# Split SiLU-multiply: each partition's rows in HBM, from one 64 KiB piece per tile to eight adjacent pieces taken by eight tiles

## The chip, the cores and the metric

The kernel runs on one core of one Trainium2 chip. The metric is the device time of one execution in microseconds; the time before is the median of three runs. A profile is one more execution, recorded by the hardware profiler.

## The reference

The input x has the shape (32, 512, 2048) in float32, 16384 rows of 8 KiB, 134.22 MB. The output has 1024 columns, 67.11 MB.

```python
def reference(x):
    half_dim = x.shape[-1] // 2
    x1, x2 = (x[..., :half_dim].copy(), x[..., half_dim:].copy())
    silu_x1 = x1 * (1 / (1 + np.exp(-x1)))
    return (silu_x1 * x2).astype(np.float32)
```

Each row is treated by itself, so it does not matter for the result which row lies on which partition, as long as the output goes to the row that the input came from.

## The kernel before

The 16384 rows are cut into 16 tiles of 1024 rows (8 MiB of x, 4 MiB of out). A tile gives K = 8 rows to each of the 128 partitions. The function `view` says which: tile i is the block of 1024 adjacent rows from row 1024 i, and partition p takes the eight adjacent rows from 8 p in it. So a partition's part of a tile is one run of 64 KiB of x, and the next partition's run follows it without a gap; a whole tile is one run of 8 MiB. In out the same holds with half the bytes, 32 KiB and 4 MiB.

There are two input buffers (`xts`) and two output buffers (`ots`), taken in turn. For each tile there is one load on SyncE's queue (in `load`, by `move`, L87), SiLU in place on the first half of each row on ScalarE (L103), the multiply with the second half into the output buffer on VectorE (L109), and one store on ScalarE's queue (in `store`, by `move`, L87). The first tile is computed in four parts and stored in five pieces (`OPENING`), which take the partitions in steps of four or two; the last is computed and stored in two parts. The other 14 tiles are each one activation, one multiply and one store.

The order on ScalarE and VectorE is written out by hand (`manual_schedule`). A load of tile i + 2 waits for the multiply of tile i, which frees its input buffer; a multiply of tile i + 2 waits for the store of tile i, which frees its output buffer. In turns of four tiles the load of tile i + 2 is ordered before or behind the store of tile i (`load_first`, `after`). Declarations of waits that are implied by others (`implied`) keep the number of semaphores down. At the end SyncE waits for the transfers to land.

Of the kernel before, what the change touches and what calls it, by code (L numbers as in the profile page):

```python
# [1 line left out]

# [4 lines left out]


@with_exitstack
def kernel(  # L10
    ctx: ExitStack,
    tc: tile.TileContext,
    x: bass.AP,
    out: bass.AP,
):


    nc = tc.nc
    P = nc.NUM_PARTITIONS

    x_flat = x.flatten_outer_dims()
    out_flat = out.flatten_outer_dims()
    num_rows, in_cols = x_flat.shape
    half = in_cols // 2
    dt = x_flat.dtype

    K = 8
    KC_EDGE = 2
    KS = 4
    OPENING = [  # L30
        (slice(0, None, 4), slice(0, 2)),
        (slice(2, None, 4), slice(0, 4)),
        (slice(2, None, 4), slice(4, None)),
        (slice(0, None, 4), slice(2, None)),
        (slice(1, None, 2), slice(None)),
    ]
    PLAN = [K] * (num_rows // (P * K))

    pool = ctx.enter_context(tc.tile_pool(name="pool", bufs=1))
    xts = [pool.tile([P, K, in_cols], dt, name=f"xt{b}") for b in range(2)]  # L40
    ots = [pool.tile([P, K, half], dt, name=f"ot{b}") for b in range(2)]

    plan = []
    row = 0
    for k in PLAN:
        plan.append((row, k))
        row += P * k
    assert row == num_rows
    n_tiles = len(plan)

    def view(flat, i):
        row0, k = plan[i]
        return flat[row0:row0 + P * k].rearrange("(p k) d -> p k d", k=k)

    ctx.enter_context(tc.manual_schedule(engines={mybir.EngineType.Activation, mybir.EngineType.DVE}))

    sent = []
    loads, stores, silus, muls = {}, {}, {}, {}

    def implied(later, earlier, reason):  # L60
        for x in later:
            for y in earlier:
                tc.declare_no_dep(x, y, reason=reason)

    def earlier(done, i):
        return [ins for j in range(i % 2, i, 2) for ins in done[j]]

    def after(later, first):
        tc.add_manual_dep(
            later,  # L70
            first.name,
            mybir.DependencyInfo(mybir.DependencyClass.NoSync, mybir.DependencyReason.DATA),
            reason="order in which the transfers take their semaphores",
        )

    def settle_all_but(n):
        rest = nc.sync.nop(nofuse=True)
        for ins in sent[:-n]:
            tc.add_manual_dep(
                rest.ins,  # L80
                ins.name,
                mybir.DependencyInfo(mybir.DependencyClass.Sync, mybir.DependencyReason.DATA),
                reason="sync sees each earlier transfer land before the last ones",
            )

    def move(queue, out, in_):
        ins = queue.dma_start(out=out, in_=in_).ins  # L87
        sent.append(ins)
        return ins

    def load(i):
        loads[i] = [move(nc.sync, xts[i % 2][:], view(x_flat, i))]
        if i >= 2:
            implied(loads[i], earlier(loads, i), "the multiplies that this load awaits came after those loads")
            implied(loads[i], earlier(silus, i), "the multiplies that this load awaits came after those activations")

    def compute(i, ot, kc):
        xt = xts[i % 2]
        silus[i], muls[i] = [], []
        for c in range(0, K, kc):  # L100
            ks = slice(c, c + kc)
            silus[i].append(
                nc.scalar.activation(  # L103
                    out=xt[:, ks, :half],
                    in_=xt[:, ks, :half],
                    func=mybir.ActivationFunctionType.Silu,
                ).ins
            )
            muls[i].append(nc.vector.tensor_mul(out=ot[:, ks], in0=xt[:, ks, :half], in1=xt[:, ks, half:]).ins)  # L109
        implied(muls[i], loads[i], "each multiply awaits an activation that came after the load")  # L110
        if i >= 2:
            implied(silus[i], earlier(silus, i), "the load that this activation awaits came after those activations")
            implied(silus[i], earlier(muls, i), "the load that this activation awaits came after those multiplies")
            implied(muls[i], earlier(muls, i), "the store that this multiply awaits came after those multiplies")

    def store(i, ot, pieces):
        ov = view(out_flat, i)
        stores[i] = [move(nc.scalar, ov[ps, ks], ot[ps, ks]) for ps, ks in pieces]

    ALL = slice(None)  # L120
    load(0)
    load(1)
    for i in range(n_tiles):
        ot = ots[i % 2]
        last = i == n_tiles - 1
        compute(i, ot, KC_EDGE if i == 0 else KS if last else K)
        pieces = [(ALL, ALL)]
        if i == 0:
            pieces = OPENING
        elif last:  # L130
            pieces = [(ALL, slice(c, c + KS)) for c in range(0, K, KS)]
        load_first = i // 4 % 2
        if load_first and i + 2 < n_tiles:
            load(i + 2)
        store(i, ot, pieces)
        if load_first and i + 2 < n_tiles:
            after(stores[i][0], loads[i + 2][0])
        if not load_first and i + 2 < n_tiles:
            load(i + 2)
            after(loads[i + 2][0], stores[i][-1])  # L140
    settle_all_but(1)


# [1 line left out]
_INS = ['x']  # L145
_OUTS = [((32, 512, 1024), 'float32')]


# [23 lines left out]
```

## Time and profile before

| what | value |
|---|---|
| median of 3 runs | 470.68 us (470.57 to 470.76) |
| profiled execution | 471.83 us |
| its span, first to last instruction | 470.1 us |
| VectorE busy | 139.3 us, 30% of the span |
| ScalarE busy | 114.1 us, 24% |
| loads' queue (q1) | 134.22 MB, 66.2% of 16 DMA engines' span |
| stores' queue (q10) | 67.11 MB, 33.1% |
| mean rate of HBM traffic | 428 GB/s over the span |
| activation of a whole tile | 7.03 us |
| multiply of a whole tile | 8.69 us |

The page gives the busy time of each engine, the share of the DMA engines in 40 slices of the span, and the queues; the trace behind it can be asked for windows of time, for waits and for the chain of work that ended last. The trace also has one record for each packet that a DMA engine moved: its start, its duration and its bytes. A load has 128 data packets of 64 KiB, a whole store 128 of 32 KiB.

### The profile page before, as it was taken

To read this page: it belongs to the slowest core of one execution; us is meant where nothing else is said; L and a number is where in the kernel's file an instruction comes from. 1 tells how busy PE (TensorE), PEld (TensorE's weight loads), DVE (VectorE), ACT (ScalarE), POOL (GpSimd) and SP (SyncE) were. 2 spreads that over 40 slices of the span, in tenths; PEclk is the share of its full clock that TensorE was granted. 3 is DMA by queue.
4 is the path that set the end of the run, shared out by engine and by line. 5 is a ranking of instruction groups with operands and counts; after the bars stand their busy time and mean duration, and the time that the engine had idled before them with its cause. 6 is when DMAs were issued, how large, how long until landed. Compare 5 with 4: busy or idle time off the path is not lost.

```text
span 470.1 us, 157 instructions
## 1 busy us (share of the span) xinstructions
DVE 139.3 (30%) x20; ACT 114.1 (24%) x21; POOL 0.2 (0%) x4
## 2 busy tenths in 40 slices
DVE  0070614307042070520605116060150702507061
ACT  1052305050040501405014050230503205032060
POOL 0000000000000000000000000000000000000000
DMA  8999999999999999999999999999999999999997
GB/s 357 446 468 424 402 441 404 415 480 402 446 402 485 407 421 427 485 407 402 443 446 443 407 443 488 393 415 443 482 407 446 404 429 460 407 446 421 424 425 336
DMA packets 4880, 201.33 MB, mean 428 GB/s; under 512 B 592, under 2 KB 592, under 8 KB 592
## 3 DMA queue, kind: packets, MB, share of 16 engines
q1 hardware_dynamic: 2304, 134.22, 66.2%
q10 hardware_dynamic: 2576, 67.11, 33.1%
HBM read 134.22 MB, written 67.11 MB: 428 GB/s over the span
## 4 chain that ended last, share of the span: by engine, by line
DMA 80%; DVE 14%; ACT 2%; DVEq 1%; issue 0%; SPq 0%
DMA out_dram<-ot 62%; DMA xt<-in_x_dram 18%; DVE ot L109 14%; ACT xt L103 2%; DVEq L167 1%; SPq L87 0%; DVEq L109 0%
## 5 line engine op out<-in xcount | busy, mean ns | idle before, releaser
L109 DVE TENSOR_TENSOR ot<-xt 128x8192 f32<-128x8192 f32 (+2 forms) x20 | 139.3, 6984 | 320.5 <-DMA out_dram<-ot 180.1
L103 ACT ACTIVATE xt<-xt 128x8192 f32<-128x8192 f32 (+2 forms) x20 | 112.8, 5661 | 339.7 <-DMA xt<-in_x_dram 339.7
L103 ACT ACT_TABLE_LOAD x1 | 1.3, 1283 | 0.7 <-PEq L156 0.7
L156 POOL MEMSET const-bfloat16-1.0<- 128x1 bf16 x1 | 0.1, 102 | 0.0
L156 POOL MEMSET const-uint8-127<- 128x1 uint8 x1 | 0.1, 102 | 0.0
L156 POOL MEMSET const-float32-0.0<- 128x1 f32 x1 | 0.1, 99 | 0.2 <-issue 0.2
L156 POOL MEMSET const-float32-1.0<- 128x1 f32 x1 | 0.1, 99 | 0.0
## 6 DMA issues: line engine op xcount, KB each, us to landing
out_dram<-ot ACTq DMA_DIRECT2D x14, 4096.0 KB, 49.2
out_dram<-ot ACTq DMA_DIRECT2D x3, 2048.0 KB, 9.4
out_dram<-ot ACTq DMA_DIRECT2D x2, 512.0 KB, 17.3
out_dram<-ot ACTq DMA_DIRECT2D x1, 768.0 KB, 28.1
xt<-in_x_dram SPq DMA_DIRECT2D x16, 42.1
out_dram<-ot ACTq DMA_DIRECT2D x1, 256.0 KB, 10.9
```

Of the source, the lines that this page charges most:

```text
L103: nc.scalar.activation(out=xt[:, ks, :half], in_=xt[:, ks, :half], func=mybir.ActivationFunctionType.Silu,).ins
L109: muls[i].append(nc.vector.tensor_mul(out=ot[:, ks], in0=xt[:, ks, :half], in1=xt[:, ks, half:]).ins)
L156: nc = _bacc.Bacc("TRN2", target_bir_lowering=False, num_devices=1)
L167: with _tile.TileContext(nc) as tc:
```

## The change

The 16 tiles remain, with the same shapes, buffers and order. `view` now cuts the 16384 rows into two groups of 8192 rows (64 MiB of x). In a group a partition owns 64 adjacent rows, 512 KiB of x, as eight pieces of eight rows; tile t of the group takes piece t of every partition. A partition's part of a tile is still one run of 64 KiB of x and 32 KiB of out, but the next partition's run now begins 512 KiB further on in x, and 256 KiB further on in out. The list of tiles with their first rows (`PLAN`, `plan`) goes, as the view works the addresses out from the tile's number.

```diff
-    PLAN = [K] * (num_rows // (P * K))
+    RUN = 8
+    n_tiles = num_rows // (P * K)
...
-    plan = []
-    row = 0
-    for k in PLAN:
-        plan.append((row, k))
-        row += P * k
-    assert row == num_rows
-    n_tiles = len(plan)
-
     def view(flat, i):
-        row0, k = plan[i]
-        return flat[row0:row0 + P * k].rearrange("(p k) d -> p k d", k=k)
+        return flat.rearrange("(g p t k) d -> g t p k d", p=P, t=RUN, k=K)[i // RUN, i % RUN]
```

## The prediction

> **What bounds the kernel now.** I read the page first, its parts 1 to 3.
>
> ```profile
> span 470.1 us, 157 instructions
> DVE 139.3 (30%) x20; ACT 114.1 (24%) x21; POOL 0.2 (0%) x4
> ...
> DMA  8999999999999999999999999999999999999997
> ...
> q1 hardware_dynamic: 2304, 134.22, 66.2%
> q10 hardware_dynamic: 2576, 67.11, 33.1%
> ```
>
> The two compute engines stand idle for over two thirds of the span. The sixteen DMA engines are busy 66.2% + 33.1% = 99.3% of it: 311.2 us with loads (queue q1) and 155.6 us with stores (q10), together 466.8 us of 470.1. The missing 3.3 us lie at the two ends of the span. So the time is the sum of the packets that one DMA engine handles, and the question is whether a packet can become shorter or longer. The view by windows says at which rate they run:
>
> ```profile
> 0.00:13.00 13.00, 0.00 (x0) 1.28 (x1) 0.20 (x4) 1.00 0.99 403
> 44.00:60.00 16.00, 8.62 (x1) 7.03 (x1) 0.00 (x0) 1.00 0.96 410
> 86.00:144.00 58.00, 17.39 (x2) 14.06 (x2) 0.00 (x0) 1.00 1.00 434
> 144.00:202.00 58.00, 16.99 (x2) 14.06 (x2) 0.00 (x0) 1.00 1.00 434
> 376.00:434.00 58.00, 17.37 (x3) 14.06 (x2) 0.00 (x0) 1.00 1.00 434
> 434.00:470.00 36.00, 9.18 (x3) 7.12 (x2) 0.00 (x0) 1.00 0.91 394
> ```
>
> The last two columns are the DMA engines' share and the GB/s. From 86 to 434 us the rate is 434 in each 58 us, whatever the mixture of loads and stores. The trace's own packet records show how flat this is: most 64 KiB load packets took 2.418 us, to the nanosecond, and most 32 KiB store packets 1.213 us. A memory that was short of something would scatter these numbers. What scatter there is lies nearly all ahead of 62 us: the first sixteen load packets (2.96 to 3.35 us, mean 3.140), and two later batches of sixteen that start together at 37 and 61 us (means 2.740 and 2.745). Summed over all packets, the time above 2.418, 1.213 and the like is 1.72 us for each engine.
>
> Last, the waits, to see who would notice a longer packet:
>
> ```profile
> ACT xt L103 <- DMA xt<-in_x_dram: 339.7, 16, 22.4
> DVE ot L109 <- DMA out_dram<-ot: 180.1, 9, 20.8
> DVE ot L109 <- ACT xt L103: 140.4, 7, 24.6
> ```
>
> ACT waits for a load before each tile, some 22 us long, and DVE for a store or for ACT. Nothing in compute can give time back: a microsecond more of packets on one engine is a microsecond more of span.
>
> **The change part by part.** The instruction streams stay as they are: each engine has the same instructions in the same order with the same shapes (16 loads of 128 x 16384 elements, 14 full stores, 7 pieces), only their source lines move up by eight. So no instruction, wait or DMA issue is added, removed or moved: cost nothing, and no cover is needed. Packet sizes stay too: a partition's part of a tile is still one run of 64 KiB of x and 32 KiB of out, and the bytes are still 134.22 + 67.11 MB. The floor stays at 128 load packets x 2.418 = 309.5 us for an engine plus its stores.
>
> What moves is the address. In a load, neighbouring partitions lay 64 KiB apart and now lie 512 KiB apart; in a store 32 KiB becomes 256 KiB. Whichever partitions the sixteen engines serve at a moment, their addresses differed by multiples of 64 KiB and now differ by multiples of 512 KiB: three more low address bits are equal in all sixteen streams, and the engines run in step, since their first packets all started within 0.4 us and then took equal times. If the memory spreads addresses over its channels by those bits, streams meet on a channel, and the packets get longer. The opening stores go over every fourth partition, so their runs lie 1 MiB apart, but they are 4.19 MB in all, 9.7 us at 434 GB/s; a tenth more there is 1 us, and I give them no term.
>
> No row of before shows a packet at the new distance, so I bound it. Below nothing: all of today's scatter goes, -1.72 us. Zero: 2.418 us as now. Above: each of the 128 load packets of an engine costs what the restarted batches cost, (2.740 + 2.745) / 2 - 2.418 = 0.324 us more, together 41.5 us; or, furthest, what the first sixteen cost, 0.722 us more, together 92.4 us. For stores the row is 1.213 us with nothing above 1.225, and their distance grows only to 256 KiB, so I take zero there. For loads I choose near the lower end, because 434 GB/s is held without scatter over 350 us, so the memory has something to spare: the restart price on one packet in eight, the first of every load, where the sixteen streams jump together by a new base. That is 16 x 0.324 = 5.2 us. It is a choice between bounds and not a measurement.
>
> One rule of the notes speaks against the change. The Trainium skill, page "DMA: Bandwidth & Descriptors", section "Latency and other measured facts", has a row on HBM row pitch at large powers of two: copies of 128 partitions x 16 KiB ran at 207 GB/s for each direction with rows 512 KiB apart, at 164 with 2 MiB and 103 with 4 MiB, against 214 with a padded pitch. The page calls channel aliasing of streams in step an inference. By its 214/207, an estimate from that page, loads alone would cost 10.5 us more and loads with stores 15.8 us, 481.2 or 486.5 us, where my sum has 5.2. No run here shows it yet.
>
> The sum: the profiled execution took 471.83 us, its span 470.1 and 1.7 us around it; it becomes 471.83 + 5.2 = 477.0. The runs shown have a median of 470.68, 1.15 lower, so I add to that: 470.68 + 5.2 = 475.9 us. Nothing new is late: each load comes 0.3 us later, ACT and DVE wait 0.3 us more for it, and the load two tiles on is released by the multiply as much later.
>
> **The rivals.** *No change.* The memory spreads these addresses as evenly as the old ones, and the DMA engine's own rate stays the bound. For it: the flat 2.418 us, and that today's distance is a power of two as well and does no harm. Against: three bits fewer to tell the streams apart. Time 470.7 us.
>
> *The collision is harder.* Streams that meet on a channel hold each other in step, so that the price falls on half or more of the load packets: 64 x 0.324 = 20.7 us gives 491.4 us, all of them 512.2 us. It decides from about one packet in four (10.4 us, 481.1 us). For it: nothing in the kernel breaks the step, since all pieces have one size. Against: the restarted batches lose their excess by the next packet, so streams here drift apart by themselves. The row on row pitch quoted above belongs to this rival, at its lower end.
>
> *Faster.* The scatter of today's first 62 us comes from addresses 64 KiB apart that meet, and the new distance parts them: at most 1.72 us, 469.0 us. It is a gain that can be measured only if over half of that, 0.94 us, goes. Against: 0.72 of it are the very first packets, which start cold together in both kernels, and the rest falls where the first stores mix in, which stays too. The rate of 434 GB/s cannot be the place of a gain, as equal packet times point to the engine and not to the address.
>
> *The change doesn't do what it says* has little room: the order of instructions and the shapes say it moves only addresses.
>
> **How the numbers follow.** A measurement of this kernel can tell about 0.2% from no change, 0.94 us, so the same is 469.7 to 471.6. Forecast, slower by 1 to 10 us: 0.45. No change: 0.34. Harder collision: 0.15. Faster: 0.06. So faster 0.06, same 0.34, slower 0.60. The time is 475.9 us, the forecast case alone 471.7 to 481. The range must take in no change below and reach into the harder collision above, where I stop at 490: 469.8 to 490 leaves out most of faster and about half of harder, some 0.13.
>
> **What would show it.** Right: the windows from 86 to 434 us show some GB/s under 434 with DMA still at full share, the share-time of q1 rises from 311.2 us by about 5, that of q10 stays at 155.6, and the packet records show longer loads at the start of each tile. No change: 434 again in each window and 2.418 us in nearly all records. Harder: long load packets throughout, and store packets above 1.213 us too. I am wrong in kind if the span grows while the DMA share falls, since then something waits that I hold to be unchanged.

## The result, and the profile after

The changed kernel takes 474.85 us (median of four runs, 474.21 to 475.34), the kernel before beside it 470.62 us (470.57 to 470.76): slower by 4.2 us, a ratio of 1.0085 with a 95% interval of 1.0072 to 1.0099. The forecast was 475.9 us and the range 469.8 to 490. The direction and nearly the size came out; where the microseconds lie did not.

The page of the profile after, parts 1 to 3 (busy time, DMA share in 40 slices, queues):

```profile
span 472.9 us, 157 instructions
DVE 139.4 (29%) x20; ACT 114.1 (24%) x21; POOL 0.2 (0%) x4
...
DMA  8999999999999999999999999999999999999987
GB/s 355 443 455 416 425 415 402 460 410 435 430 455 407 452 438 410 441 441 460 413 441 416 432 441 421 430 466 438 407 424 468 407 438 438 446 407 452 416 380 299
...
q1 hardware_dynamic: 2304, 134.22, 66.0%
q10 hardware_dynamic: 2576, 67.11, 32.9%
```

Compute is as it was. Stores take 32.9% of 472.9 us, 155.6 us of an engine on average, the same as before. The loads' share, 66.0%, is too round for a small difference; the packet records, summed, give 311.9 us of loads for a mean engine against 311.4 before, 0.6 us more. So the sum of packets of a mean engine grew by less than a microsecond, and a sum over the mean does not explain the 4.2. The windows of after (share and GB/s last):

```profile
60.00:86.00 26.00, 7.38 (x2) 7.03 (x1) 0.00 (x0) 1.00 0.98 416
86.00:144.00 58.00, 17.29 (x3) 14.06 (x2) 0.00 (x0) 1.00 1.00 434
...
202.00:260.00 58.00, 16.78 (x3) 14.06 (x2) 0.00 (x0) 1.00 1.00 433
...
376.00:434.00 58.00, 17.39 (x3) 14.06 (x2) 0.00 (x0) 1.00 1.00 434
```

From 86 to 434 us the rate is again 433 to 434 in each window. What is left stands ahead of 86 us and at the end, seen with other windows. Before:

```profile
60.00:100.00 40.00, 8.76 (x2) 7.94 (x2) 0.00 (x0) 1.00 1.01 433
...
468.00:475.00 7.00, 0.00 (x0) 0.00 (x0) 0.00 (x0) 1.00 0.01 2
```

After:

```profile
60.00:100.00 40.00, 9.46 (x2) 7.03 (x1) 0.00 (x0) 1.00 0.99 422
...
468.00:475.00 7.00, 0.00 (x0) 0.00 (x0) 0.00 (x0) 1.00 0.17 70
```

From 60 to 100 us the view has 422 GB/s where the kernel before had 433. It books each packet whole to the window in which the packet starts, so most of that gap comes from the edges (the shares are 0.99 and 1.01); with each packet spread over its duration the rates are 427 and 430, only 0.3 us of transfer on average. At the end the difference is plain: a few engines still move data (70 GB/s) when the kernel before is done.

The trace's packet records say which engines. They don't name the engine, but each engine starts a packet when its last one ends, so they can be strung into sixteen chains; each chain then holds 12.58 MB but for a few swapped packets, so what follows on a single chain is approximate. Time above the flat 2.418 and 1.213 us, by chain: in before fourteen chains lost 1.4 to 1.8 us in all, nearly all of it ahead of 62 us. In after ten chains lost 1.3 to 1.8 us, and six lost 2.7 to 5.2 us. Most of what these six lost beyond the others lies between 60 and 100 us (some 1.4 to 2.0 us in each), in single packets, mostly 0.1 to 0.7 us too long. The slowest of them moves its last byte at 471.8 us. Most of the rest end near 469.1 us; those that were on time had nothing to do for 1.3 to 1.9 us before the last two stores, as the last load is there only when its slowest engine has brought its share, and the last multiply waits for it. In before most chains end at 467.5 to 467.8 us. So the 4.2 us are about 1.5 (all wait for the last load) plus 2.7 (the slowest engine ends behind the rest).

The profiled execution of before, 471.83 us, was 1.2 us over its median, and its records show why: one chain there ended at 468.9 us, 1.3 behind the rest. That is why the two spans differ by 2.8 us and the medians by 4.2.

### The profile page after: what moved, and what is told of

It reads as the page before. It is cut to its first block, busy times and chain, and to the rows that moved or that the text cites. A ratio compares the mean times of both kernels' runs of the same rounds, so it can differ in the third digit from the quotient of the medians.

```text
span 472.9 us, 157 instructions
## 1 busy us (share of the span) xinstructions
DVE 139.4 (29%) x20; ACT 114.1 (24%) x21; POOL 0.2 (0%) x4
## 3 DMA queue, kind: packets, MB, share of 16 engines
q10 hardware_dynamic: 2576, 67.11, 32.9%
## 4 chain that ended last, share of the span: by engine, by line
DMA 80%; DVE 14%; ACT 2%; DVEq 1%; issue 0%; SPq 0%
DMA out_dram<-ot 62%; DMA xt<-in_x_dram 18%; DVE ot L101 14%; ACT xt L95 2%; DVEq L159 1%; SPq L79 0%; DVEq L101 0%
```

## The experiments

Theories at the start. A: streams that read in step at equal low address bits meet; a few engines lose time, and the last one sets the end. B: any distance between the partitions' pieces costs, whatever its bits. C: the stores do it. D: the new addresses are slow when first reached. E came later: the price depends on how many engines read such addresses at once. Edits are against the changed kernel unless another is named.

**Each half alone.** Only loads with the new distance:

```diff
     def view(flat, i):
+        if flat is out_flat:
+            return flat[i * P * K:(i + 1) * P * K].rearrange("(p k) d -> p k d", k=K)
         return flat.rearrange("(g p t k) d -> g t p k d", p=P, t=RUN, k=K)[i // RUN, i % RUN]
```

> Loads as after (partitions 512 KiB apart), stores as before (32 KiB apart, a tile one run of 4 MiB), so output rows land at other places than the reference's. Theory A (streams in step with equal low address bits meet on the read side; a few DMA engines lose 1 to 3 us each between 60 and 100 us, and the last of them sets the end): 473.5 to 476 us, 64 KiB packets above 2.44 us beyond 62 us on a few engines. Rival C (it is the stores' 256 KiB distance): 470.6 us and no such packets.

Measured: 474.6 us, 1.0068 (1.0044 to 1.0091); three chains lost 4.3 to 4.9 us, and data still moves at the end:

```profile
468.00:475.00 7.00, 0.00 (x0) 0.00 (x0) 0.00 (x0) 1.00 0.18 75
```

Only stores with it (the same lines with `x_flat`):

> The other half: loads as before (64 KiB apart), stores as after (256 KiB apart); output rows land at other places than the reference's. Theory A (reads): 470.6 us, within 0.9. Rival C (stores): 473.5 to 476 us. If each half shows a part, or neither, the two must meet each other, and then reads against writes is the cause and not reads among themselves.

Measured: 471.39 us, 1.0009 (0.9995 to 1.0023), which is not told from no change. From 62 us on 97 packets took some 0.05 us more than the flat time, spread over all chains, and no chain ended over 1 us behind the others. No packet starts after 468 us:

```profile
468.00:475.00 7.00, 0.00 (x0) 0.00 (x0) 0.00 (x0) 1.00 0.00 0
```

The loads carry the loss; theory C falls.

**Power of two or distance.** One group of 16 tiles (1 MiB in x, 512 KiB in out), against one of 15 tiles and a single dense one (960 and 480 KiB):

```diff
-    RUN = 8
+    RUN = 16
```

> One group of 16 tiles: loads 1 MiB apart, stores 512 KiB apart. Theory A: one more address bit is equal, so more than after: 477 to 490 us, more packets above 2.44 us, perhaps store packets above 1.23 us now. Rival B (distance as such): 474 to 476 us, about as after.

Measured: 491.99 us (487.69 to 495.4, the ratio without the longest 1.0409, 1.0349 to 1.0468), a little over what was expected. The page of that longest execution (DMA share and rate in 40 slices of 12.3 us):

```profile
span 493.6 us, 157 instructions
...
DMA  9999999999999999999999999999999999999957
GB/s 335 345 341 343 341 329 361 430 420 443 425 438 438 428 422 430 449 422 438 428 435 433 433 428 422 430 438 428 449 420 433 438 428 425 433 438 428 422 223 327
```

For seven slices the rate is 329 to 361 with the engines fully busy, and then, up to the last two slices, it is 420 to 449. Long packets, and no waits; all of them are loads, as no whole store's packet took over 1.225 us. The 15-tile group, against the changed kernel:

```diff
     def view(flat, i):
-        return flat.rearrange("(g p t k) d -> g t p k d", p=P, t=RUN, k=K)[i // RUN, i % RUN]
+        first = 0
+        for run in (15, 1):
+            if i < first + run:
+                rows = flat[first * P * K:(first + run) * P * K]
+                return rows.rearrange("(p t k) d -> t p k d", t=run, k=K)[i - first]
+            first += run
```

> One group of 15 tiles with pieces 960 KiB apart in x (480 KiB in out), and one tile as before. Beside the kernel with 16 tiles to a group (1 MiB apart, 487.7 to 495.4 us) the distance is 6% less, but no longer a power of two. Theory A (equal low address bits): 470.6 to 473 us. Rival B (distance as such): 486 to 494 us.

Measured: 470.59 us, 1.0001 (0.9984 to 1.0018). The windows of its profile, whose execution took 472.74 us:

```profile
60.00:86.00 26.00, 7.39 (x2) 7.03 (x1) 0.00 (x0) 1.00 1.00 425
86.00:144.00 58.00, 17.41 (x3) 14.06 (x2) 0.00 (x0) 1.00 1.00 434
144.00:202.00 58.00, 17.38 (x3) 14.06 (x2) 0.00 (x0) 1.00 1.00 434
```

Six percent less distance, and 21 us are gone. Theory B falls: what costs at 1 MiB is not the distance as such but that it is a large power of two.

Half the distance of after, `RUN = 4` (256 KiB in x, 128 KiB in out):

> Groups of 4 tiles: loads 256 KiB apart, stores 128 KiB. Theory A: one address bit less in common than after, so less: 470.6 to 472.5 us. Rival B (distance as such, any tile that is not one dense run): 474 to 476 us, as after.

Measured: 472.56 us (472.41 to 472.86), 1.0036 (1.0027 to 1.0046), a little above what A expected. With 64, 256, 512 and 1024 KiB between pieces of x the times are 470.6, 472.6, 474.9 and 492.0 us.

**Other odd distances.** Loads 520 KiB apart, stores as after:

```diff
     def view(flat, i):
+        if flat is x_flat:
+            g, t = divmod(i, RUN)
+            pitch = RUN * K + 1
+            row0 = g * (num_rows - P * pitch)
+            rows = flat[row0:row0 + P * pitch].rearrange("(p r) d -> p r d", r=pitch)
+            return rows[:, t * K:(t + 1) * K]
```

> As after, but the partitions' pieces of x lie 520 KiB apart (65 rows) in place of 512 KiB, with the stores as after (256 KiB); the second group of tiles begins 1 MiB earlier so as to fit, so some rows of x are read twice and some not at all. Theory A (equal low address bits): the loss goes, 470.6 us within 0.9, or a little less if the early scatter goes too. Rival B (any distance between the pieces costs, whatever its bits): 474 to 476 us as after.

Measured: 472.48 us (472.07 to 473.99), 1.0031 (1.0015 to 1.0046): some 2.4 us less than after, but not the 470.6 expected. In its profile, of the longest of ten executions (473.99), one chain alone lost over 4 us. With `pitch = (RUN + 1) * K`, 576 KiB:

> As the kernel with loads 520 KiB apart, but 576 KiB (72 rows, nine pieces of which eight are read), stores as after (256 KiB); again some rows of x are read twice and some not at all. 520 KiB gave 472.48 us. If what was left there came of an offset of 8 KiB that parts the streams too little, 576 KiB, as 960 KiB did, brings the time to that of the stores' half alone: 470.8 to 471.7 us. If it comes of the stores and the loads meeting, whatever the loads' bits: 472.2 to 473 us again.

Measured: 472.26 us, 1.0024 (1.0010 to 1.0038), from 471.13 to 473.8 over ten runs; in the profile, again of the longest (473.8), one chain lost over 4 us and the others no more than before. One late chain stands in the profile of the 960 KiB kernel too (472.74 us, where its median is 470.59), so these profiles don't say what the median lost. The first expectation is missed by half a microsecond. That 8 KiB is too small an offset was thus not the reason. What remains at 520 and 576 KiB, 1.4 to 1.7 us over before, is not explained; 960 KiB does not show it, but it also had other stores. So at 512 KiB the power of two accounts for some 2.4 to 2.6 of the 4.2 us, and the rest is open.

**The price of one late engine**, by itself: the kernel before, with four small loads of one partition ahead.

```diff
     load(0)
+    for k in range(4):
+        move(nc.scalar, ots[1][k:k + 1], x_flat[k * 4:(k + 1) * 4].rearrange("(p r) (k d) -> p (r k) d", p=1, k=2))
     load(1)
```

> The kernel before with four small loads of one partition ahead (32 KiB each, into the second output buffer before its first use), so that one DMA engine has 4 x 1.213 = 4.85 us more to move and the other fifteen nothing. If the last engine sets the end of each load and store, the time is 474.5 to 476 us, with a stretch of 1 to 2 us before the last two stores in which the other engines are idle. If the engines share work among them, 470.9 us (4.85 / 16 = 0.3 more).

Measured: 476.12 us (475.71 to 476.34), 1.0111 (1.0085 to 1.0137): 0.13 MB, 0.07% of the bytes, cost 5.4 us. The end of its profile:

```profile
434.00:458.00 24.00, 7.32 (x2) 6.73 (x2) 0.00 (x0) 1.00 0.92 397
458.00:468.00 10.00, 5.68 (x2) 0.39 (x1) 0.00 (x0) 1.00 0.82 347
468.00:475.00 7.00, 0.00 (x0) 0.00 (x0) 0.00 (x0) 1.00 0.29 122
```

The share falls to 0.92 and 0.82 at the end and data still moves after 468 us, the same mark as in after. Fifteen chains end at 470.1 us, one at 472.7, where before ends near 467.6. The other engines took over none of the late one's work: what one engine loses, the kernel loses. This settles the last part of theory A; the cost is 0.6 us above the 4.85, and the time 0.1 above the expected range.

**Is it the step?** The 16-tile group (`RUN = 16`) with six small loads that were to set the engines apart:

```diff
...
     load(0)
+    first = 0
+    for k in (2, 5, 7, 10, 12, 15):
+        rows = x_flat[2 * first:2 * (first + k)].rearrange("(p r) (k d) -> p (r k) d", r=2, k=2)
+        move(nc.scalar, ots[1][first:first + k, 0:4], rows)
+        first += k
     load(1)
```

> The 16-tile group (1 MiB apart) with six small loads ahead, on 2, 5, 7, 10, 12 and 15 partitions of the second output buffer, which is unused until then: each moves 16 KiB for as many DMA engines, so that the engines begin the first load up to 6 x 0.61 = 3.7 us out of step. Theory A with the engines' step as its condition: the slow stretch of the first 86 us (323 to 355 GB/s) is gone or much shorter, with over 410 GB/s there, and the time 473 to 480 us, of which some 4 us are the extra bytes on the engine with most of them. Rival D (the new addresses are slow to be reached the first time, whoever comes when): the slow stretch stays, 490 to 499 us.

Measured: 495.17 us (490.5 to 497.19), 1.05 (1.0438 to 1.0561). Its windows:

```profile
13.00:44.00 31.00, 7.19 (x4) 7.31 (x4) 0.00 (x0) 1.00 1.00 350
44.00:60.00 16.00, 1.70 (x1) 2.40 (x1) 0.00 (x0) 1.00 1.00 416
60.00:86.00 26.00, 8.69 (x1) 4.63 (x1) 0.00 (x0) 1.00 0.99 381
86.00:144.00 58.00, 17.38 (x2) 14.06 (x2) 0.00 (x0) 1.00 1.01 427
```

While mostly loads run (13 to 44 us) it is as slow as without the small loads (347 there), and the time is the one that rival D gave. But the run does not test the step. Load 0 does not wait for them, and in the records only two of the 51 small packets come ahead of its first packets; the others go in between its later ones and the next load's, the last at 37 us, and at 13.8 us all sixteen engines start a large packet within 0.8 us. Nor do the records of the 16-tile group without small loads show engines in step: ahead of 45 us the sixteen start their packets over 0.9 to 2.7 us, and the packets are long all the same. That streams must be in step to pay is not shown.

That led to theory E. In the records of the 16-tile kernel, load packets took 0.03 us too long on average with 12 engines or fewer loading (counted at the middle of the packet), 0.16 with 14 and 0.66 with 16. Early on nearly all sixteen load; from 100 us on loads and stores alternate among the engines, and 14 or more load at once in only 8% of the time (in before 62%, at no cost). But the same records part number from time, and against E: ahead of 86 us packets with 12 or fewer loading lost 0.46 us too, and from 100 us on those with 14 or more lost 0.02, no more than the rest. In a run for this question, stores were left out but for the last tile's two:

```diff
-    RUN = 8
+    RUN = 16
...
-        store(i, ot, pieces)
-        if load_first and i + 2 < n_tiles:
+        if last:
+            store(i, ot, pieces)
+        else:
+            stores[i] = []
+        if last and load_first and i + 2 < n_tiles:
             after(stores[i][0], loads[i + 2][0])
         if not load_first and i + 2 < n_tiles:
             load(i + 2)
-            after(loads[i + 2][0], stores[i][-1])
```

> The 16-tile group (1 MiB apart) with all stores left out but the last tile's two, so that from 2 to the end of the loads only loads are in flight. Theory E (the price depends on how many engines read aligned addresses at once, and mixing with stores is the cure): the loads stay slow to their end, 330 to 370 GB/s in every window, 134.22 MB in 363 to 407 us, the time 385 to 430 us. Theory A (it is paid only until the engines have drifted out of step) and D (first touch): slow for the first 60 to 90 us alone and 434 GB/s after it, the time 345 to 360 us.

Measured: 367.8 us (two runs, 366.45 and 369.15), between the two expectations.

```profile
13.00:44.00 31.00, 8.90 (x4) 7.31 (x4) 0.00 (x0) 1.00 1.02 368
44.00:86.00 42.00, 14.56 (x2) 14.06 (x2) 0.00 (x0) 1.00 0.99 379
86.00:144.00 58.00, 20.20 (x3) 20.53 (x3) 0.00 (x0) 1.00 0.99 392
144.00:202.00 58.00, 26.07 (x3) 15.72 (x4) 0.00 (x0) 1.00 0.98 397
202.00:260.00 58.00, 26.08 (x3) 19.98 (x3) 0.00 (x0) 1.00 0.98 409
260.00:310.00 50.00, 17.38 (x2) 18.24 (x3) 0.00 (x0) 1.00 0.98 380
```

The loads recover by themselves in part (packets 0.46 us too long on average from 24 to 60 us, 0.10 to 0.25 later), but never to the rate that the full kernel has from 86 us on. So stores in between help, and how they do is open. The number of loading engines alone does not set the price: with sixteen loading nearly all the time a packet lost 0.23 us here, against 0.66 in the full kernel. First touch (D) doesn't fit: the price lasts through all sixteen tiles. The controls, 960 KiB and the changed kernel's 512 KiB without stores:

> The same without stores for the 15-tile group (960 KiB apart, one tile dense): the control at nearly the same distance. Every theory but distance as such: 434 GB/s all along, 134.22 MB in 310 us, the time 333 to 337 us. Rival B (distance): slow as with 1 MiB.

> The changed kernel (512 KiB apart) without its stores, the last tile's two excepted. Theory E: its price with all engines reading is small, as its first 24 us show (3 ns on a load packet): 430 to 434 GB/s, the time 333 to 340 us. If the loss of the changed kernel comes of reads alone over time, rate under 425 GB/s and 340 to 350 us.

Measured: 341.37 and 342.08 us (two runs each). Both lie above what was expected, the second in the range that was set for a loss by reads alone; but the control at 960 KiB has the same loss, 5.2 us of long load packets on a mean engine in both (1.7 in before), and in both the chains stand idle for some 0.5 to 4 us while a load waits for its buffer. So without stores 512 KiB costs no more than 960 KiB, and 960 KiB is not free either; the dense order without stores was not run. As the engines wait for each other in those pauses, an engine that falls behind might not show here. Why the changed kernel's packets get long just from 60 to 100 us stays open.

## Why the prediction was right or wrong

- *The bound, and that compute and the order of instructions do not matter.* Right: the compute rows, q10's 155.6 us and the flat 434 GB/s from 86 us on are unchanged.
- *Three more equal address bits make streams meet, on the read side, nothing for stores.* Right about the side, and shown: the loads' half alone gives 474.6 us, the stores' half 471.39 us, not told from no change. That equal address bits are the reason is shown at 1 MiB, whose loss 960 KiB undoes, and at 512 KiB for some 2.5 of the 4.2 us. That streams meet on a channel, or that they must run in step for it, no run shows.
- *5.2 us as 0.324 us on the first packet of each load, on every engine.* This term is the step that failed. A mean engine lost about 0.6 us more than before in its load packets, not 5.2. The first packets of the fifteen later loads lost some 0.1 us of an engine in all, where the term has 0.324 for each; the long packets that came on top lie mostly between 60 and 100 us. The price itself came from batches at 37 and 61 us in the midst of loads, while the first packets of the later loads lost 0.04 us in all in before, so its rows did not bear out the place; a third batch, at 52 us and some 2.6 us a packet, was passed over. And the last engine lost 5.2 us where before's lost 1.4 to 2.6. That the number 5.2 came near the measured 4.2 is luck: the time goes by the slowest engine and not by the mean, and two errors, a price too high and an engine too typical, went against each other.
- *"A microsecond more of packets on one engine is a microsecond more of span."* Right, and more important than I used it for: 4.85 us on one engine alone cost 5.4.
- *The windows from 86 to 434 us under 434, q1 up by about 5 us.* Wrong on both: 433 to 434, and 0.6 us.
- *No change:* excluded by the interval. *Faster:* the scatter ahead of 62 us stayed, as argued. *Harder collision:* not at 512 KiB, but it is what 1 MiB does, with 0.4 to 0.8 us on a mean load packet until 86 us.
- The Trainium skill, page "DMA: Bandwidth & Descriptors", section "Latency and other measured facts", was right in direction; its 207 against 214 GB/s at 512 KiB would have been 481.2 or 486.5 us here, by the estimate in the prediction, and 474.85 was measured. Its remedy, to pad the row pitch by a few KiB, agrees in part with the run at 520 KiB, 8 KiB more, which took back 2.4 of the 4.2 us; 960 KiB, which took back all that 1 MiB costs, is further off the power of two than that.

## What to carry to other kernels

When DMA engines are the bound, count the slowest engine and not the mean: here the other engines took over none of a late engine's work (4.85 us more on one engine cost 5.4), and a few long packets on one engine moved the end of the kernel. A layout that gives partitions pieces at a power-of-two distance can cost time even when each piece is long and contiguous and every instruction stays the same: 1.9 us at 256 KiB, 4.2 at 512 KiB and 21 at 1 MiB in this kernel; if such a layout is wanted, try a group of 15 tiles instead of 16. Look at GB/s by window: a rate below the usual one at full DMA share meant long packets here, and a falling share at the end a late engine. Take wide windows for it, as each packet counts where it starts: one 64 KiB packet of each engine is 1 MB, some 6% of what moves in 40 us.

## What the runs showed of the hardware that was not expected

- A 64 KiB packet takes 2.418 us to the nanosecond at any of the distances, in most packets (1858 of 2048 in before, 1518 with 1 MiB between pieces); the loss is in stretches and not everywhere.
- With 1 MiB between pieces the rate was 329 to 361 GB/s for the first 86 us and 420 to 449 after it, in the same execution with the same pattern of addresses. With stores left out it stayed at 368 to 410. What brings the recovery about is not shown.
- The kernel before has executions up to 2.4 us over its fastest (470.58 to 472.94 in twenty), and its profiled one shows a single late engine, as does that of the 960 KiB kernel; a profile that is slower than the median may hold nothing but that.
